# Order of high and low weight parts, and modulation sums of two column groups per call, in a two-block transformer kernel

## The chip, the cores and the metric

One core of a Trainium2 chip runs one program of about 39,000 instructions. The metric is the device time of one execution in microseconds, the median of the runs shown. A profile holds one execution.

## What is computed

The reference runs two blocks on 256 tokens of width 2048, in float32. The first block has two layers and a second stream, the context, of 256 tokens as well. In each layer the input is scaled and shifted by a modulation that comes from a vector `c` (for the tokens) and `c_ctx` (for the context):

```python
sh_l, sc_l, g_l = jnp.split(jax.nn.silu(c) @ w_mod[l] + b_mod[l], 3, axis=-1)
sh_c, sc_c, g_c = jnp.split(jax.nn.silu(c_ctx) @ w_mod[l] + b_mod[l], 3, axis=-1)
hl = xl * (1.0 + sc_l[:, None, :]) + sh_l[:, None, :]
parts_l = jnp.split(hl @ w_in[l], SPLIT_POINTS, axis=-1)
```

Then come a short convolution, differential attention and a pooling, a product with `w_out`, a residual gated by `g_l` or `g_c`, and a layer norm. The second block has a norm, two attentions of eight heads, gated products `w_proj_a`, `w_proj_b` and `w_out`, and a feed-forward part with `w_up` and `w_down` of width 8192.

## The kernel before

The weights are streamed from HBM once, in chunks of 512 KB: two row blocks of 128 (`CHUNK = 2`) by 512 columns, or four row blocks by 256. `fetch` (line 169) issues the transfer on SP's queue, lets ACT copy the chunk to a high part in float32r (line 184) and DVE subtract to get the low part (line 185). Two chunks are made ahead of the one in use (`LOOKAHEAD`); raw, high and low tiles have three buffers each. A product of float32 accuracy is the sum of three float32r products: high by high, high by low, low by high.

Two functions multiply. `lin_b` (line 250) takes the weights as the stationary operand and gives the result transposed, four blocks of 128 columns in four accumulators. With 256 tokens it folds the two products of the high weights into one: high and low parts of the activations stand side by side as 512 columns, so each row block of each column block is a product of 512 columns (line 266) and one of 256 columns with the low weights (line 268), one after the other. With 512 tokens it calls `mm3` (line 245), three products of 512 columns. `lin_a` (line 278) takes the activations as the stationary operand and the weights as the moving one, with `mm3` as well: 512 columns, or 256 in the last two column blocks of `w_out` and of the last `w_down`. In the second layer and the second block nearly all of `lin_b` is folded. The first layer works on 512 tokens.

The order of the chunks is one list, `stream`, filled ahead of the work by `plan` and `weave` (lines 145 and 148). `weave` puts chunks of the modulation's weights `w_mod` between those of the main products: one by one in the first layer, one for three in the second. `side` (line 195) runs twice per chunk; it hands modulation chunks to their step function and counts down the list `deferred`, whose entries run when their count reaches zero. `bg_step` advances attention and norms between chunks.

The first column groups of the first layer's modulation go through PE directly (`mod_first`, line 365). All others go through `mod_side` (line 403), a job of one group `nt` of 512 columns. For each row of a chunk DVE multiplies by the column of `silu(c)` and adds into an accumulator `ma0` for the context and `ma1` for the tokens (lines 416 and 418). When the last chunk is done, `deferred` holds `cols` for shift and scale or `gate` for the gate, due after five calls of `side`. Both sum over the 128 partitions by a product with a 128 by 32 tile of ones, one per stream, into rows 0 to 31 and 32 to 63 of one tile `aux` (lines 428 and 446). `cols` copies 64 rows back (line 430), and two calls later `finish` transposes four blocks of 128 columns on PE (line 435) and sets the columns (line 436). `gate` loads 64 rows of `b_mod` on ACT's queue (line 442), adds it on DVE stream by stream (line 448) and writes one row per stream to HBM (line 449).

The jobs are: two single groups for the first layer's scale and shift (line 909), four gate groups of both streams for the first layer (`side0`), eight scale and shift groups for the second (`side1`, in the order of `NTS`, line 456), and four gate groups of the token stream alone (`side2`). The accumulators have one buffer each. A tile of the pool `qs` (ten buffers of 544 columns) serves input pieces, high and low parts of the heads, the pooling and four rows of the forget gate. Its column sums lie in a tile `fc` of its own (line 1157).

Of the kernel before, what the change touches and what calls it, by code (L numbers as in the profile page):

```python
# [12 lines left out]
F32 = mybir.dt.float32  # L13
# [48 lines left out]
def tile_two_blocks(ctx: ExitStack, tc: tile.TileContext, a: dict, out: bass.AP, blocks: dict):  # L62
# [14 lines left out]
    p_qs = pool("qs", 10)  # L77
# [167 lines left out]
    def mm3(ps, lh, ll, rh, rl, start, stop):  # L245
        mm(ps, lh, rh, start=start, stop=False)  # L246
        mm(ps, lh, rl, start=False, stop=False)  # L247
        mm(ps, ll, rh, start=False, stop=stop)  # L248

    def lin_b(act, tok, consume, ncols=512, korder=K16, mid=None):  # L250


        ntok = tok.stop - tok.start
        fold = 2 * ntok == 512
        nb = [(b * P, min(P, ncols - b * P)) for b in range((ncols + P - 1) // P)]
        ps = [acc() for _ in nb]
        for k0 in korder:
            hi, lo = wget()
            last = k0 == korder[-1]
            nk = hi.shape[1]  # L260
            for (c, w), p in zip(nb, ps):
                for kk in range(nk):
                    ah, al = act[k0 + kk]
                    start, stop = k0 == korder[0] and kk == 0, last and kk == nk - 1
                    if fold:
                        mm(p[:w, :].rearrange("p (a t) -> p a t", a=2), hi[:, kk, c:c + w], act.both(k0 + kk, tok),  # L266
                           start=start, stop=False)
                        mm(p[:w, :ntok], lo[:, kk, c:c + w], ah[:, tok], start=False, stop=stop)  # L268
                    else:
                        mm3(p[:w, :ntok], hi[:, kk, c:c + w], lo[:, kk, c:c + w], ah[:, tok], al[:, tok], start, stop)  # L270
                if last:
                    consume(c // P, (p[:w].rearrange("p (a t) -> p t a", a=2),) if fold else p[:w, :ntok])
            side()
            bg_step()
            if mid:
                mid(k0)

    def lin_a(act, tiles, consume, korder=K16, mid=None, hold=1, lead=0, hook=None):
# [4 lines left out]
        for ks in [korder[:lead]][:lead] + [[k] for k in korder[lead:cut]] + [korder[cut:]]:  # L283
# [119 lines left out]
    def mod_side(l, nt, streams=(0, 1), wait=5):  # L403

        st = {}

        def fn(k0):
            def step(raw):
                if k0 == 0:
                    for s in streams:  # L410
                        st[s] = p_ma.tile([P, 512], F32, tag=f"ma{s}", name=f"ma{s}")
                for kk in range(CHUNK):
                    k = k0 + kk
                    for s in streams:
                        if k == 0:
                            V.tensor_scalar(st[s], raw[:, kk, :], cc2[:, k, s:s + 1], None, op0=ALU.mult)
                        else:
                            V.scalar_tensor_tensor(st[s], raw[:, kk, :], cc2[:, k, s:s + 1], st[s], op0=ALU.mult,  # L418
                                                   op1=ALU.add)
                if k0 == K16[-1]:  # L420
# [3 lines left out]

        def cols():
            ps = aux()
            for s in streams:
                mm(ps[32 * s:32 * s + 32, :], ones, st[s], start=True, stop=True)
            r = st[0][:64]
            S.copy(r, ps[:64])  # L430

            def finish():
                pt = aux()[:, :256].rearrange("p (b r) -> p b r", b=4)
                for b in range(4):
                    nc.tensor.transpose(pt[:, b, :], r[:, b * P:(b + 1) * P], ident[:64, :64])
                set_cols(l, nt // 4, nt % 4 * 4, 4, pt.rearrange("p b (s t) -> p b s t", s=2)[:, :, :, 0])
            deferred.append([2, finish])

        def gate():
            o = (nt - 8) * 512  # L440
            br = tmp()
            S.dma_start(br[:64], bass.AP(tensor=a["b_mod"].tensor, offset=a["b_mod"].offset + l * 3 * D + 2 * D + o,
                                         ap=[[0, 64], [1, 512]]))
            ps = aux()
            for s in streams:
                mm(ps[32 * s:32 * s + 32, :], ones, st[s], start=True, stop=True)
            for s in streams:
                V.tensor_add(br[32 * s:32 * s + 32], ps[32 * s:32 * s + 32, :], br[32 * s:32 * s + 32])
                S.dma_start(grow[l][s:s + 1, o:o + 512], br[32 * s:32 * s + 1])
        return entries(("w_mod", l), nt * 512, 512, K16, fn)  # L450


# [3 lines left out]
    NTS = [nt for j in range(4) for nt in (j, 4 + j)]  # L456
# [446 lines left out]
    for j, (kt, n) in enumerate(GROUPS):  # L903
        w = [e for name, g in L_FIRST for e in entries(("w_in", 0), O[name] + 512 * g, 512, range(kt, kt + n, CHUNK),
                                                   nk=min(n, CHUNK))]
        if j + 1 < len(GROUPS):
            nxt = GROUPS[j + 1]
            if n == 4:
                m0, m1 = mod_side(0, nxt[0] // 4, wait=2), mod_first(1, *nxt, ("act",))
# [232 lines left out]
    fc = cst.tile([P, T], F32, name="fc")  # L1142
# [275 lines left out]
```

## Time and profile before

| | us |
|---|---|
| median of 3 runs | 2888.54 |
| lowest and highest | 2886.82, 2889.2 |
| the profiled execution | 2888.59 |
| its span, first to last instruction | 2886.8 |

| engine | busy us | share |
|---|---|---|
| PE, matmuls | 2857.0 | 99% |
| PEld, weight loads | 2371.6 | 82% |
| DVE | 2003.2 | 69% |
| ACT | 1159.7 | 40% |
| POOL | 222.5 | 8% |

PE is TensorE, DVE VectorE, ACT ScalarE, POOL GpSimd, SP SyncE. A row of the timeline has the start in us, the duration in us, engine, line, operation, output and inputs, the shape (stationary operand by moving operand) and a count. The end of a matmul is modelled and overlaps the start of the next one, so the pace is read from starts. A row of one line gives the count, the least, median and greatest duration in ns and the starts of the first and the last instruction in the stretch.

### The profile page before, as it was taken

Reading aid. Unit: us, or ns where it says so; the run is one execution under the profiler, and the core shown is the slowest. Engines: PE = TensorE matmul, PEld = TensorE weight load, DVE = VectorE, ACT = ScalarE, POOL = GpSimd, SP = SyncE. Lnnn points to the kernel's source line nnn. Section 1 sums busy time; section 2 is a strip of 40 time slices with the busy share of each in tenths; the row PEclk is TensorE's granted clock in tenths of the full one; section 3 lists DMA queues with packets and bytes.
Section 4 is the critical chain, followed back from the end, with each engine's and each line's share of the span. In section 5 each row is a group of like instructions: output and inputs, shape, how many; then the busy total and the mean of one; then the engine's idle time right before and its main releaser. Section 6 shows DMA issues by size and latency. Waiting matters only on the chain.

```text
span 2886.8 us, 39022 instructions
## 1 busy us (share of the span) xinstructions
PE 2857.0 (99%) x14970; PEld 2371.6 (82%) x14970; DVE 2003.2 (69%) x3061; ACT 1159.7 (40%) x1620; POOL 222.5 (8%) x284
## 2 busy tenths in 40 slices
PE   8999999999999999999999999999999999999998
PEld 6777787777879788888888888888888888888887
DVE  5889987887975658467676666776656656565564
ACT  3223432432312435245445443544444444344443
POOL 0000001001100410011100000001101001010011
PEclk9999999999999999999999999999999999999999
DMA  9764455445764445445756555455656656656555
GB/s 332 275 211 142 135 173 165 147 163 178 246 197 134 135 137 194 157 161 192 244 168 194 182 157 188 156 188 184 204 183 189 191 189 188 194 181 196 190 188 168
DMA packets 150532, 533.89 MB, mean 185 GB/s; under 512 B 17204, under 2 KB 21052, under 8 KB 149320
## 3 DMA queue, kind: packets, MB, share of 16 engines
q1 hardware_dynamic: 142752, 510.79, 54.3%
q0 software_dynamic: 5632, 18.36, 2.1%
q10 hardware_dynamic: 1960, 2.24, 0.3%
q8 instruction: 117, 1.92, 0.3%
q14 instruction: 71, 0.58, 0.1%
HBM read 527.09 MB, written 4.23 MB: 184 GB/s over the span
## 4 chain that ended last, share of the span: by engine, by line
PE 76%; DVE 2%; issue 2%; DMA 1%; ACT 1%; POOL 0%; POOLq 0%; ACTq 0%; DVEq 0%
PE acc L266 23%; PE acc L246 12%; PE acc L248 12%; PE acc L247 12%; PE acc L268 12%; PE aux L670 1%; PE aux L702 1%; DVE lo L185 1%; DVE ma L418 1%; PE aux L692 0%; PE aux L1184 0%; ACT hi L184 0%; DMA raw<-in_w_in_dram 0%; DMA raw<-in_w_out_dram 0%; PE aux L1214 0%
## 5 line engine op out<-in xcount | busy, mean ns | idle before, releaser
L185 DVE TENSOR_TENSOR lo<-raw,hi 128x1024 fp32r<-128x1024 f32 (+1 forms) x774 | 947.0, 1226 | 646.3 <-ACT hi L184 645.2
L184 ACT CAST hi<-raw 128x1024 fp32r<-128x1024 f32 (+1 forms) x774 | 808.4, 1045 | 1419.1 <-PE acc L248 447.8
L266 PE MATMUL acc<-act,hi 128*128 128x512 f32 x2960 | 1048.1, 399 | 0.4 <-DVE qs L308 0.4
L268 PE MATMUL acc<-act,lo 128*128 128x256 f32 x2960 | 828.3, 280 | 0.0
L266 PEld LDWEIGHTS acc<-act,hi 128*128 128x128 f32 x2960 | 554.1, 187 | 139.7 <-issue 5.1
L246 PE MATMUL acc<-hi,act 128*128 128x512 f32 (+1 forms) x1568 | 584.2, 373 | 2.7 <-ACT act L350 1.7
L247 PE MATMUL acc<-lo,act 128*128 128x512 f32 (+1 forms) x1568 | 578.6, 369 | 1.1 <-DVE lo L185 1.1
L248 PE MATMUL acc<-hi,act 128*128 128x512 f32 (+1 forms) x1568 | 578.6, 369 | 0.1
L268 PEld LDWEIGHTS acc<-act,lo 128*128 128x128 f32 x2960 | 556.9, 188 | 1.9 <-DVE lo L185 0.3
L418 DVE SCALAR_TENSOR_TENSOR ma<-mod,cc,ma 128x512 f32<-128x512 f32 x480 | 339.5, 746 | 26.2 <-DMA mod<-in_w_mod_dram 24.8
L246 PE MATMUL acc<-act,hi 128*128 128x512 f32 x896 | 356.9, 398 | 0.2 <-ACT hi L184 0.2
L247 PE MATMUL acc<-act,hi 128*128 128x512 f32 x896 | 350.2, 391 | 0.0
L248 PE MATMUL acc<-act,lo 128*128 128x512 f32 x896 | 350.1, 391 | 0.0
L246 PEld LDWEIGHTS acc<-hi,act 128*128 128x128 f32 x1568 | 296.5, 189 | 56.9 <-issue 4.0
L248 PEld LDWEIGHTS acc<-hi,act 128*128 128x128 f32 x1568 | 296.2, 189 | 51.5 <-DVE act L351 1.5
L247 PEld LDWEIGHTS acc<-lo,act 128*128 128x128 f32 x1568 | 296.6, 189 | 50.5 <-DVE lo L185 2.5
L246 PEld LDWEIGHTS acc<-act,hi 128*128 128x128 f32 x896 | 168.6, 188 | 46.1 <-issue 8.8
L248 PEld LDWEIGHTS acc<-act,lo 128*128 128x128 f32 x896 | 168.5, 188 | 35.9 <-issue 0.4
L247 PEld LDWEIGHTS acc<-act,hi 128*128 128x128 f32 x896 | 168.7, 188 | 33.5 <-issue 0.5
L317 DVE TENSOR_REDUCE tmp<-acc 128x256 f32<-128x512 f32 x185 | 124.3, 684 | 57.3 <-PE acc L268 57.3
L1292 POOL TENSOR_TENSOR tmp<-tmp 128x256 f32<-128x256 f32 x64 | 53.0, 828 | 573.3 <-DVE tmp L1291 566.6
L678 ACT ACTIVATE pp<-aux,small 128x512 f32<-128x512 f32 (+1 forms) x96 | 58.3, 613 | 55.1 <-DVE small L674 55.0
(217 smaller groups left out, 1655.0 us busy)
## 6 DMA issues: line engine op xcount, KB each, us to landing
raw<-in_w_in_dram SPq DMA_DIRECT2D x379, 512.0 KB, 4.0
mod<-in_w_mod_dram SPq DMA_DIRECT2D x152, 512.0 KB, 3.7
raw<-in_w_up_dram SPq DMA_DIRECT2D x128, 512.0 KB, 4.1
raw<-in_w_down_dram SPq DMA_DIRECT2D x128, 512.0 KB, 4.2
raw<-in_w_out_dram SPq DMA_DIRECT2D x96, 512.0 KB, 4.3
mod<-in_w_mod_dram SPq DMA_DIRECT2D x8, 2048.0 KB, 13.5
raw<-in_w_proj_a_dram SPq DMA_DIRECT2D x16, 512.0 KB, 4.1
raw<-in_w_proj_b_dram SPq DMA_DIRECT2D x16, 512.0 KB, 4.3
```

Source lines behind the costliest of these rows:

```text
L184: S.copy(hi, raw)
L185: (fn or V).tensor_sub(lo, raw, hi)
L246: mm(ps, lh, rh, start=start, stop=False)
L247: mm(ps, lh, rl, start=False, stop=False)
L248: mm(ps, ll, rh, start=False, stop=stop)
L266: mm(p[:w, :].rearrange("p (a t) -> p a t", a=2), hi[:, kk, c:c + w], act.both(k0 + kk, tok), start=start, stop=False)
L268: mm(p[:w, :ntok], lo[:, kk, c:c + w], ah[:, tok], start=False, stop=stop)
L317: V.reduce_sum(t, ps[0], axis=AX.X)
L418: V.scalar_tensor_tensor(st[s], raw[:, kk, :], cc2[:, k, s:s + 1], st[s], op0=ALU.mult, op1=ALU.add)
L670: mm(p[:, :nk], a[r, q0:q0 + P], b[r, 0:nk], start=n == 0, stop=n == 2)
L678: S.activation(t, ps[i][:, :nk], AF.Exp, bias=nm[:, i:i + 1], scale=QK_SCALE, accum_out=sums[:, i:i + 1])
L1292: G.tensor_mul(t, t, t)
```

## The change

In `lin_b` and `lin_a` the products of a chunk that use the high weights come first and those that use the low weights last. In `lin_b` this goes over all column blocks in the middle chunks and by column block in the first and the last chunk. `mod_side` takes a list of column groups; their accumulators stay until the last group's last chunk, and then one call sums up to four of them, on rows 0 to 127 of `aux`, followed by one copy, four transposes and one `set_cols` per group. Gates are paired as (8, 9) and (10, 11), scale and shift of the second layer as (j, 4 + j). The two single groups of the first layer stay single. The pool `qs` has nine buffers, and `fc` uses the accumulator `ma0`.

```diff
-    p_qs = pool("qs", 10)
+    p_qs = pool("qs", 9)
...
-    def mm3(ps, lh, ll, rh, rl, start, stop):
-        mm(ps, lh, rh, start=start, stop=False)
-        mm(ps, lh, rl, start=False, stop=False)
-        mm(ps, ll, rh, start=False, stop=stop)
...
-            for (c, w), p in zip(nb, ps):
-                for kk in range(nk):
-                    ah, al = act[k0 + kk]
-                    start, stop = k0 == korder[0] and kk == 0, last and kk == nk - 1
-                    if fold:
-                        mm(p[:w, :].rearrange("p (a t) -> p a t", a=2), hi[:, kk, c:c + w], act.both(k0 + kk, tok),
-                           start=start, stop=False)
-                        mm(p[:w, :ntok], lo[:, kk, c:c + w], ah[:, tok], start=False, stop=stop)
-                    else:
-                        mm3(p[:w, :ntok], hi[:, kk, c:c + w], lo[:, kk, c:c + w], ah[:, tok], al[:, tok], start, stop)
-                if last:
-                    consume(c // P, (p[:w].rearrange("p (a t) -> p t a", a=2),) if fold else p[:w, :ntok])
+
+            pairs = list(zip(nb, ps))
+            for g in ([[x] for x in pairs] if last or k0 == korder[0] else [pairs]):
+                for (c, w), p in g:
+                    for kk in range(nk):
+                        ah, al = act[k0 + kk]
+                        wt, start = hi[:, kk, c:c + w], k0 == korder[0] and kk == 0
+                        if fold:
+                            mm(p[:w, :].rearrange("p (a t) -> p a t", a=2), wt, act.both(k0 + kk, tok), start=start,
+                               stop=False)
+                        else:
+                            mm(p[:w, :ntok], wt, ah[:, tok], start=start, stop=False)
+                            mm(p[:w, :ntok], wt, al[:, tok], start=False, stop=False)
+                for (c, w), p in g:
+                    for kk in range(nk):
+                        mm(p[:w, :ntok], lo[:, kk, c:c + w], act[k0 + kk][0][:, tok], start=False,
+                           stop=last and kk == nk - 1)
+                    if last:
+                        consume(c // P, (p[:w].rearrange("p (a t) -> p t a", a=2),) if fold else p[:w, :ntok])
...
+                    tt, p = slice(t * P, (t + 1) * P), ps[i][:, :n]
                     for kk in range(nk):
-                        ah, al = act[k0 + kk]
-                        mm3(ps[i][:, :n], ah[:, t * P:(t + 1) * P], al[:, t * P:(t + 1) * P], hi[:, kk], lo[:, kk],
-                            k0 == korder[0] and kk == 0, k0 == korder[-1] and kk == nk - 1)
+                        for j, x in enumerate(act[k0 + kk]):
+                            mm(p, x[:, tt], hi[:, kk], start=k0 == korder[0] and kk == j == 0, stop=False)
+                    for kk in range(nk):
+                        mm(p, act[k0 + kk][0][:, tt], lo[:, kk], start=False, stop=k0 == korder[-1] and kk == nk - 1)
...
-    def mod_side(l, nt, streams=(0, 1), wait=5):
+    def mod_side(l, nts, streams=(0, 1), wait=5):
+        jobs = [(nt, s) for nt in nts for s in streams]
...
+                        j = jobs.index((nt, s))
+                        st[nt, s] = p_ma.tile([P, 512], F32, tag=f"ma{j}", name=f"ma{j}")
...
+                if (nt, k0) == (nts[-1], K16[-1]):
                     deferred.append([wait, cols if nt < 8 else gate])
...
+        n = 32 * len(jobs)
+        def sums():
+            ps = aux()
+            for j, job in enumerate(jobs):
+                mm(ps[32 * j:32 * j + 32, :], ones, st[job], start=True, stop=True)
+            return ps
         def cols():
-            ps = aux()
-            for s in streams:
-                mm(ps[32 * s:32 * s + 32, :], ones, st[s], start=True, stop=True)
-            r = st[0][:64]
-            S.copy(r, ps[:64])
+            ps = sums()
+            r = st[jobs[0]][:n]
+            S.copy(r, ps[:n])
             def finish():
-                pt = aux()[:, :256].rearrange("p (b r) -> p b r", b=4)
+                pt = aux()[:, :4 * n].rearrange("p (b r) -> p b r", b=4)
                 for b in range(4):
-                    nc.tensor.transpose(pt[:, b, :], r[:, b * P:(b + 1) * P], ident[:64, :64])
+                    nc.tensor.transpose(pt[:, b, :], r[:, b * P:(b + 1) * P], ident[:n, :n])
...
         def gate():
...
+            for j, (nt, s) in enumerate(jobs):
+                o = (nt - 8) * 512
+                S.dma_start(br[32 * j:32 * j + 32],
+                            bass.AP(tensor=a["b_mod"].tensor, offset=a["b_mod"].offset + l * 3 * D + 2 * D + o,
+                                    ap=[[0, 32], [1, 512]]))
+            ps = sums()
+            V.tensor_add(br[:n], ps[:n], br[:n])
...
-    side0 = [e for nt in range(8, 12) for e in mod_side(0, nt)]
-    side1 = [e for nt in NTS for e in mod_side(1, nt)]
-    side2 = [e for nt in range(8, 12) for e in mod_side(1, nt, (1,))]
+    side0 = [e for nt in (8, 10) for e in mod_side(0, (nt, nt + 1))]
+    side1 = [e for j in range(4) for e in mod_side(1, (j, 4 + j))]
+    side2 = [e for nt in (8, 10) for e in mod_side(1, (nt, nt + 1), (1,))]
...
-    fc = cst.tile([P, T], F32, name="fc")
+    fc = p_ma.tile([P, 512], F32, tag="ma0", name="fc")[:, :T]
```

## Rows read from the trace of the kernel before

**Rows 1.** Page, part 1: busy time, share of the span, count of each engine.

```profile
PE 2857.0 (99%) x14970; PEld 2371.6 (82%) x14970; DVE 2003.2 (69%) x3061; ACT 1159.7 (40%) x1620; POOL 222.5 (8%) x284
```

**Rows 2.** Waits of PE: engine line waited for, total us, times, longest us.

```profile
PE aux L670 <- ACT pp L678: 2.0, 1, 2.0
...
PE acc L247 <- DVE lo L185: 1.1, 2, 0.9
```

**Rows 3.** Busy time of each engine in one stretch, us.

```profile
core 0: us, PE busy (x) PEld busy (x) DVE busy (x) ACT busy (x) POOL busy (x), PEclk, DMA share, GB/s
200.00:300.00 100.00, 99.00 (x455) 77.97 (x454) 96.03 (x177) 35.24 (x56) 5.78 (x8) 1.00 0.47 149
```

**Rows 4.** Line 248 in a stage of 512-column products, w_down of group 0.

```profile
L248 PE MATMUL acc<-hi,act x128: 389/389/398, 2257.2 to 2343.6; 128*128 128x512 f32 x128
```

**Rows 5.** Timeline of PE, 512 then 256 columns: start, us, engine, line, instruction.

```profile
2854.39 0.39 PE L248 MATMUL acc<-hi,act 128*128 128x512 f32 x1
2854.62 0.28 PE L246 MATMUL acc<-hi,act 128*128 128x256 f32 x1
...
2854.85 0.28 PE L248 MATMUL acc<-hi,act 128*128 128x256 f32 x1
...
2857.49 0.28 PE L246 MATMUL acc<-hi,act 128*128 128x256 f32 x1
```

**Rows 6.** Line 268 in two stretches of the alternating order.

```profile
L268 PE MATMUL acc<-act,lo x256: 277/281/284, 2344.1 to 2434.2; 128*128 128x256 f32 x128
...
L268 PE MATMUL acc<-act,lo x148: 274/277/280, 1898.9 to 1949.9; 128*128 128x256 f32 x148
```

**Rows 7.** Timeline of PE where 512-column products follow 256-column ones.

```profile
2434.30 0.40 PE L246 MATMUL acc<-hi,act 128*128 128x512 f32 x1
...
2434.77 0.39 PE L248 MATMUL acc<-hi,act 128*128 128x512 f32 x1
...
2435.69 0.39 PE L246 MATMUL acc<-hi,act 128*128 128x512 f32 x1
```

**Rows 8.** Calls of sums: two in the chain, two in the timeline of PE.

```profile
547.19 0.98 PE aux L428 x4
...
1363.78 0.97 PE aux L446 x2
...
1167.25 1.05 PE L446 MATMUL aux<-ma,ones 128*32 128x512 f32 x2
1168.22 0.50 PE L246 MATMUL acc<-hi,act 128*128 128x512 f32 x1
1168.56 0.39 PE L247 MATMUL acc<-lo,act 128*128 128x512 f32 x1
...
171.71 1.92 PE L379 MATMUL aux<-mod,csil 128*32 128x512 f32 x16
173.56 0.50 PE L246 MATMUL acc<-act,hi 128*128 128x512 f32 x1
```

**Rows 9.** Timeline of PE: four transposes from 64 rows, four from 128.

```profile
136.30 0.39 PE L248 MATMUL acc<-act,lo 128*128 128x512 f32 x1
136.62 0.46 PE L435 MATMUL aux<-ident,ma 64*128 64x64 f32 x4
137.01 0.50 PE L246 MATMUL acc<-act,hi 128*128 128x512 f32 x1
...
653.05 0.60 PE L718 MATMUL aux<-ident,tmp 128*128 128x128 f32 x4
653.40 0.48 PE L246 MATMUL acc<-act,hi 128*128 128x512 f32 x1
```

**Rows 10.** Groups by line: count, busy us, mean ns, idle before.

```profile
L266 PE MATMUL acc<-act,hi 128*128 128x512 f32 x2960 | 1048.1, 399 | 0.4 <-DVE qs L308 0.4
...
L428 PE MATMUL aux<-ma,ones 128*32 128x512 f32 x40 | 10.5, 603 | 0.0
...
L446 PE MATMUL aux<-ma,ones 128*32 128x512 f32 x24 | 8.4, 604 | 0.0
```

More of the change, by code (lines that the diff above doesn't have):

```diff
@@ L401, in mod_first, with fn @@
         return res
-    def mod_side(l, nt, streams=(0, 1), wait=5):
+    def mod_side(l, nts, streams=(0, 1), wait=5):
+        jobs = [(nt, s) for nt in nts for s in streams]
         st = {}
-        def fn(k0):
+        def fn(nt, k0):
             def step(raw):
@@ L414, in step @@
                     for s in streams:
+                        t = st[nt, s]
                         if k == 0:
-                            V.tensor_scalar(st[s], raw[:, kk, :], cc2[:, k, s:s + 1], None, op0=ALU.mult)
+                            V.tensor_scalar(t, raw[:, kk, :], cc2[:, k, s:s + 1], None, op0=ALU.mult)
                         else:
-                            V.scalar_tensor_tensor(st[s], raw[:, kk, :], cc2[:, k, s:s + 1], st[s], op0=ALU.mult,
-                                                   op1=ALU.add)
-                if k0 == K16[-1]:
+                            V.scalar_tensor_tensor(t, raw[:, kk, :], cc2[:, k, s:s + 1], t, op0=ALU.mult, op1=ALU.add)
+                if (nt, k0) == (nts[-1], K16[-1]):
                     deferred.append([wait, cols if nt < 8 else gate])
@@ L437, in cols @@
+                for i, nt in enumerate(nts):
+                    set_cols(l, nt // 4, nt % 4 * 4, 4,
+                             pt.rearrange("p b (i s t) -> p i b s t", s=2, t=32)[:, i, :, :, 0])
             deferred.append([2, finish])
         def gate():
-            o = (nt - 8) * 512
             br = tmp()
-            S.dma_start(br[:64], bass.AP(tensor=a["b_mod"].tensor, offset=a["b_mod"].offset + l * 3 * D + 2 * D + o,
-                                         ap=[[0, 64], [1, 512]]))
@@ L444, in gate @@
[L444 to L450, printed above, removed]
+            for j, (nt, s) in enumerate(jobs):
[3 more added lines that the diff above has]
+                                    ap=[[0, 32], [1, 512]]))
@@ L453, in tile_two_blocks @@
+            ps = sums()
+            V.tensor_add(br[:n], ps[:n], br[:n])
+            for j, (nt, s) in enumerate(jobs):
+                o = (nt - 8) * 512
+                S.dma_start(grow[l][s:s + 1, o:o + 512], br[32 * j:32 * j + 1])
+        return [e for nt in nts for e in entries(("w_mod", l), nt * 512, 512, K16, lambda k0, nt=nt: fn(nt, k0))]
     O = dict(cu=0, cb=512, cc=1024, cg=1536, q=2048, k=3072, v=4096, ag=5120, pu=6144, pg=6656)
@@ L455, in tile_two_blocks @@
     L_REST = [("cc", 0), ("v", 1), ("k", 1), ("q", 1), ("ag", 1), ("cb", 0), ("cg", 0), ("pu", 0), ("pg", 0)]
-    NTS = [nt for j in range(4) for nt in (j, 4 + j)]
     GROUPS = [(0, 1), (1, 1), (2, 2), (4, 4), (8, 4), (12, 4)]
@@ L908, in tile_two_blocks @@
             if n == 4:
-                m0, m1 = mod_side(0, nxt[0] // 4, wait=2), mod_first(1, *nxt, ("act",))
+                m0, m1 = mod_side(0, (nxt[0] // 4,), wait=2), mod_first(1, *nxt, ("act",))
                 m = m0[:4] + m1[:1] + m0[4:] + m1[1:]
```

2 lines of the change are left out of this document (removed).

## The prediction

> **What bounds the kernel now.** I read the engines' shares first: PE is busy 99% of the span, DVE 69%, ACT 40% [rows 1]. Matmul ends are modelled, so that share alone proves little. The second view is who waited for whom on PE: the longest single wait after the start is 2.0 us, and all waits for a low part come to 1.1 us [rows 2]. The third is the stretch by engine: even where DVE is fullest, 96%, PE is busy 99% [rows 3]. So PE's own stream is the bound nearly everywhere. What takes time there is the distance from one matmul's start to the next one's, and that I took from first and last starts.
>
> In a stage of 512-column products alone 128 rounds of three stand between 2257.2 and 2343.6, which is 86.4 / 127 / 3 = 0.2268 us a step [rows 4]. In a run of 256-column products 23 starts span 2854.85 to 2857.49, 0.1200 us a step [rows 5]. A high and a low product at those two steps are 0.3468 us. The alternating order of `lin_b` (512, 256, 512, 256) needs 90.1 / 255 = 0.3533 us a pair in one whole stage and 51.0 / 147 = 0.3469 us in another stretch [rows 6]. Three more whole stages of 256 pairs ran at the slow step; I take two thirds slow, a mean of 0.351. That is the slack part 1 can touch.
>
> **Part 1, order of high and low.** No product, weight load or column is added or removed: 2960 pairs before and after [rows 10]. Of their chunks 268 are middle ones (42 products of 8 chunks with 6 each, 8 of 4 chunks with 2 each) and 100 are first or last.
>
> A middle chunk becomes eight 512-column products and then eight of 256. At the pure steps that is 8 x 0.3468 = 2.774 us. Two changes of shape come with it. Into 256 columns the first two steps take 0.23 us instead of 0.24 [rows 5], so 0.01 is gained. Back into 512 the first six take 1.39 us, 2434.30 to 2435.69 [rows 7], against 6 x 0.2268 = 1.36, so 0.03 is lost. Net 2.794 us, against 8 x 0.351 = 2.808 now: 0.014 x 268 = 3.8 us gained. Bounds: if all pairs already ran at 0.3469, the switches lose 0.02 x 268 = 5.4 us; if the switches were free, 0.034 x 268 = 9.1 are gained. I take the middle, since both switches stand in the trace.
>
> A first or last chunk goes by column block, two of 512 and two of 256. Two 512s after a switch take 0.47 us [rows 7], two 256s 0.23 [rows 5], together 0.70 against 0.702 now. 400 such blocks give 0.8 us gained, with bounds of 2.6 lost and 3.4 gained.
>
> With four or more high products ahead of it, a low part that is late no longer stops PE. The waits that can go are 1.1 us [rows 2]; I take 1. What is late next is the high part, which ACT makes and this order does not help. A high buffer now comes free after 8 of 16 products, so ACT's next cast may start up to a microsecond earlier; the low buffer is held to the chunk's end as before. No engine gets more work, and I cost that at nothing.
>
> In `lin_a` and in the 512-token products of the first layer all steps are 512 columns (or 256) whatever the order, so the order costs nothing there; the bounds are the waits just named.
>
> **Part 2, sums of the modulation.** There are 18 calls of the sums now: 10 of two streams (40 records in pairs of passes) and 8 gates, of which 4 have two streams and 4 one (24 records) [rows 10]. After it there are 10: 2 single column groups of the first layer, 4 pairs of the second layer, 2 + 2 pairs of gates. Eight fall away.
>
> Each lasts 0.98 us with two streams and 0.97 with one [rows 8], so the streams run side by side. Around it the stream loses more: entering a narrower shape takes 0.32 us instead of 0.227 [rows 9], and the first product behind takes 0.34 (1168.22 to 1168.56) instead of 0.227 [rows 8]. Alone a call thus costs 0.97 + 0.09 + 0.11 = 1.17 us, beside other auxiliary work 0.98. I take 1.1: 8 x 1.1 = 8.8 us gained, bounds 7.8 and 9.4.
>
> Four streams in a call should cost what two do. Eight products on four quadrants, 16 records, take 173.56 - 171.71 = 1.85 us [rows 8], two batches of about 0.93. So nothing is added. The Trainium skill, page TensorE: Matmul & The Clock Gate, section Measured speedup vs the span model, lists 3.07 times for four row tiles, not 4; by it a call of four would be longer by a third, and six such calls would give back some 2 us as an estimate. The row shows no such loss, and I go by it.
>
> The transposes behind go from ten groups to six. Such a group now takes 0.39 us (136.62 to 137.01), enters late by 0.09 [rows 9] and leaves by 0.11, 0.59 together. A group on 128 rows, as the four new ones will be, takes 0.35 (653.05 to 653.40) and needs no narrower shape on the way in [rows 9]; with the exit 0.46. So 10 x 0.59 - 2 x 0.59 - 4 x 0.46 = 2.9 us gained.
>
> Elsewhere: DVE's gate additions go from 12 to 4, ACT's copies from 10 to 6; both lie beside PE and are worth nothing while PE bounds. ACT issues 12 loads of b_mod instead of 8, in front of the hi casts queued behind them; the gate's addition waits for the last, and the low parts stand behind it on DVE. The cover is two chunks made ahead. Between nothing and one worst wait of 2.0 us [rows 2] for each of four gates I take 0.5 us lost. The first column group of a pair waits eight chunks longer for its sums, but the last pair ends where the last group did, and only it is awaited. The next accumulators wait for the transposes half as often. The ninth instead of tenth qs buffer and the shared tile for fc are reused long after their last readers; a head's four tiles take those of two heads before. I cost them at nothing; with that cover gone, a wait of 2.0 us at each of the two pooling stages, 4 us.
>
> **The sum.** 3.8 + 0.8 + 1 + 8.8 + 2.9 - 0.5 = 16.8 us less. The profiled execution took 2888.59 us, 1.8 beyond its span of 2886.8, and stands 0.05 above the median of the three runs. 2888.6 - 16.8 = 2871.8, so **2872 us**.
>
> **Rivals.** *The order doesn't matter to the step* (0.19): the present 0.353 comes from something else, such as where the weights lie, and remains. For it: the same alternating order ran at 0.347 too, without any change in code. Then part 1 gives only its 1 us: 2888.6 - 12.2 = 2876. The Trainium skill, same page, section Back-to-back issue gap, has N / 2.4 + 2.5 ns for a warm step, which no order changes; 216 and 109 ns by that rule, and the rows here are above it.
>
> *Runs without a price for the switch* (0.15): all 2960 pairs go at 0.3468, 12.4 us instead of 4.6: 2864. For it: one of the two switches gains. Against: the 0.03 us back into 512 columns.
>
> *The freed time becomes waits* (0.13): the calls of the first layer lie where DVE is fullest, up to 96% [rows 3]. PE would wait for lo parts instead. Then part 2 is lost and part 1 remains, 2888.6 - 5.1 = 2883.5. Against: there too PE waits for low parts 1.1 us at most [rows 2].
>
> *Slower: each change between runs drains PE* (0.07). Place: the switch between high and low run. If it cost what entering and leaving the narrow shape do, 0.1 us [rows 8, 9], 268 x 2 + 100 x 8 = 1336 switches are 134 us, less the 12.4 and the other 12.2: about 2998. The sign turns at 24.6 / 1336 = 18 ns a switch. Against: the rows give -10 and +30 ns, a mean of 10, and the +30 is cut short where a run has two products.
>
> *The change doesn't do what it says*: four quadrants are not side by side and six calls keep their double length. That gives 6 us back, 2878; 0.06, and it lies within the range.
>
> **How the numbers follow.** The forecast has 0.40; its own range is 2863 to 2880 from the bounds above. 0.2% is about what a measurement of this kernel can tell from no change, 5.8 us: faster is under 2882.8. Forecast, the neutral order, the free switch and the serial quadrants all lie there, with 0.80. The lost time counts as no change, 0.13. The drained switch is slower, 0.07. The range goes from the free switch with a slow step everywhere before, 2960 x 0.0065 = 19.2 and the other 12.2 (2857), to the case of lost time and a microsecond or two beyond (2885).
>
> **What would show it.** In the profile after: a step of about 0.227 inside eight high and 0.120 inside eight low products of a middle chunk; w_up stages of 256 pairs shorter than 90.1 us by about half a microsecond; 10 calls of sums, of the same 0.98 us; six groups of transposes; no wait for lo on PE. The forecast is wrong if the first steps of each run are far over 0.24 us, if a call on four quadrants takes over 1.2, or if waits for ACT's hi, DVE or aux appear where the calls were.

## The result, and the profile after the change

The changed kernel took a median of 2873.85 us (2871.32 to 2876.18, 4 runs), beside 2888.87 for the kernel before on the same chip: a ratio of 0.9949, 95% interval 0.9932 to 0.9966, 15.0 us less. 2872 was forecast, in a range of 2857 to 2885. In the third set of experiments it ran again: 2871.10 (5 runs) beside 2887.70, ratio 0.9937 [0.9923, 0.995], 16.6 less. So the total of 16.8 came out. Several of its terms did not, as the traces and the runs below show. The profiled execution of the first set is the longest of its four, 2876.18 us; that of the third is the second shortest of its five, 2867.47.

The page of the changed kernel, part 1, answers to [rows 1]: PE's busy time is 20 us less with nearly the same count, and DVE has as much to do as before.

```profile
PE 2836.9 (99%) x14954; PEld 2373.3 (83%) x14954; DVE 2006.9 (70%) x3053; ACT 1156.3 (40%) x1618; POOL 217.9 (8%) x284
```

The order, in the timeline of PE in a w_up stage, two middle chunks (start, length, line, and how many instructions the row holds):

```profile
2345.56 2.00 PE L264 MATMUL acc<-act,hi 128*128 128x512 f32 x8
2347.40 1.11 PE L271 MATMUL acc<-act,lo 128*128 128x256 f32 x8
2348.35 2.00 PE L264 MATMUL acc<-act,hi 128*128 128x512 f32 x8
2350.19 1.12 PE L271 MATMUL acc<-act,lo 128*128 128x256 f32 x8
```

From one run of eight highs to the next it is 2348.35 - 2345.56 = 2.79 us a chunk, where 2.794 was forecast: 1.84 for the highs and 0.95 for the lows. The low products of a whole w_up stage and of the stretch that had run fast before, by line:

```profile
L271 PE MATMUL acc<-act,lo x256: 274/283/283, 2334.9 to 2423.6; 128*128 128x256 f32 x128
...
L271 PE MATMUL acc<-act,lo x146: 274/283/283, 1889.3 to 1939.7; 128*128 128x256 f32 x146
```

The stage needs 88.7 us between its first and last low product, where it was 90.1 [rows 6]; the other row needs 50.4 for 146 pairs, 0.348 a pair, where it was 0.347. What ran slowly gained, and what ran fast lost a little.

The sums and the transposes behind them, in PE's timeline, a pair of column groups of the second layer and its transposes, answer to [rows 8, 9]:

```profile
659.21 1.06 PE L437 MATMUL aux<-ma,ones 128*32 128x512 f32 x8
660.21 0.50 PE L267 MATMUL acc<-act,hi 128*128 128x512 f32 x1
660.55 0.39 PE L268 MATMUL acc<-act,hi 128*128 128x512 f32 x1
...
665.79 0.60 PE L448 MATMUL aux<-ident,ma 128*128 128x128 f32 x4
666.15 0.48 PE L267 MATMUL acc<-act,hi 128*128 128x512 f32 x1
666.46 0.40 PE L268 MATMUL acc<-act,hi 128*128 128x512 f32 x1
```

Four streams take 660.21 - 659.21 = 1.00 us; two took 0.98 [rows 8]. The first product behind takes 0.34, as before. The transposes from 128 rows take 0.36, and 0.31 for the first product behind.

PE's waits in the changed kernel, whole span (engine, line, what it waited for: total us, times, longest us):

```profile
PE aux L651 <- DVE tmp L647: 6.8, 2, 4.5
...
PE aux L685 <- ACT pp L693: 3.3, 2, 2.7
```

No wait for a low part (L185) is left in the whole list. The first row is new: the pool product of `do_pu` waits for DVE, 2.3 us in the first layer's pooling stage and 4.5 in the second's; in the kernel before it was 0.8 us, once, in the second:

```profile
PE aux L636 <- DVE tmp L632: 0.8, 1, 0.8
```

The row L685 is the attention's wait of [rows 2] at its new line.

The second layer's pooling stage grew from 63.8 us (1344.1 to 1407.9) to 68.2 (1332.4 to 1400.6). It is counted here, in every kernel, over the last 320 products into `acc` ahead of the next stage (the second half of `do_cg`, then `do_pu` and `do_pg`), from the start of the first of them to the first product of the next stage. Waits of DVE and POOL in that stretch:

```profile
DVE tmp L646 <- DMA tmp<-in_invc_dram: 5.1, 2, 4.7
...
POOL qs L628 <- DVE tmp L646: 12.7, 1, 12.7
```

In the kernel before, DVE's wait for the factors is shorter there, and POOL has none at the pads:

```profile
DVE tmp L631 <- DMA tmp<-in_invc_dram: 1.0, 1, 1.0
```

By line, the loads of the averaging factors (643, from issue to landing), the clearing of the pads (628) and the row loads (865); the landing in us, the others in ns of the shortest, median and longest, then first and last start in us:

```profile
DMA to landing us min/median/max: 3.8/3.8/8.8
...
L628 POOL MEMSET qs<- x3: 105/124/124, 1357.8 to 1370.6; 128x8 f32 x3
...
L865 POOL DMA_DIRECT2D p<-in_ln_g_dram x4: 538/538/538, 1370.9 to 1372.5; - x4
```

In the kernel before the same three clearings went out within 0.2 us:

```profile
L613 POOL MEMSET qs<- x3: 125/127/128, 1367.8 to 1368.0; 128x8 f32 x3
...
L850 POOL DMA_DIRECT2D p<-in_ln_g_dram x4: 538/538/538, 1368.0 to 1369.6; - x4
```

With nine buffers one pad has to wait until DVE's multiplication has read the old buffer. POOL stands at it for 12.7 us, and the row loads queued behind go out 38.5 us into the stage, not 24. There they overlap the factors' loads in time, one of which takes 8.8 us to land; DVE waits for it, and PE for DVE.

### The profile page after: what moved, and what is told of

The parts are those of the page before. It is cut to its first block, busy times and chain, and to the rows that moved or that the text cites. A ratio compares the mean times of both kernels' runs of the same rounds, so it can differ in the third digit from the quotient of the medians.

```text
span 2874.4 us, 39003 instructions
## 1 busy us (share of the span) xinstructions
PE 2836.9 (99%) x14954; PEld 2373.3 (83%) x14954; DVE 2006.9 (70%) x3053; ACT 1156.3 (40%) x1618; POOL 217.9 (8%) x284
## 4 chain that ended last, share of the span: by engine, by line
PE 85%; DVE 7%; DMA 3%; issue 3%; ACT 1%; POOL 0%; SPq 0%; POOLq 0%; ACTq 0%; DVEq 0%
PE acc L264 23%; PE acc L297 20%; PE acc L271 17%; PE acc L299 10%; PE acc L267 6%; PE acc L268 6%; DMA mod<-in_w_mod_dram 2%; DVE ma L426 2%; DVE lo L185 1%; PE aux L685 1%; PE aux L717 1%; PE aux L383 1%; PE aux L707 1%; DVE small L687 0%; DMA tmp<-in_invc_dram 0%
## 5 line engine op out<-in xcount | busy, mean ns | idle before, releaser
L185 DVE TENSOR_TENSOR lo<-raw,hi 128x1024 fp32r<-128x1024 f32 (+1 forms) x774 | 950.9, 1232 | 663.9 <-ACT hi L184 591.4
L264 PE MATMUL acc<-act,hi 128*128 128x512 f32 x2960 | 800.0, 395 | 0.1
L297 PE MATMUL acc<-hi,act 128*128 128x512 f32 (+1 forms) x3136 | 768.9, 370 | 2.5 <-ACT act L354 1.4
L271 PE MATMUL acc<-act,lo 128*128 128x256 f32 (+1 forms) x3856 | 709.2, 307 | 0.0
L271 PEld LDWEIGHTS acc<-act,lo 128*128 128x128 f32 x3856 | 612.9, 189 | 92.4
L297 PEld LDWEIGHTS acc<-hi,act 128*128 128x128 f32 x3136 | 548.3, 189 | 104.5 <-ACT hi L184 3.0
L264 PEld LDWEIGHTS acc<-act,hi 128*128 128x128 f32 x2960 | 509.2, 188 | 74.8 <-issue 1.5
L299 PE MATMUL acc<-lo,act 128*128 128x512 f32 (+1 forms) x1568 | 438.3, 368 | 0.1
L267 PE MATMUL acc<-act,hi 128*128 128x512 f32 x896 | 358.7, 400 | 0.2 <-ACT hi L184 0.2
L268 PE MATMUL acc<-act,hi 128*128 128x512 f32 x896 | 352.4, 393 | 0.0
L267 PEld LDWEIGHTS acc<-act,hi 128*128 128x128 f32 x896 | 169.7, 189 | 44.1 <-issue 7.7
L268 PEld LDWEIGHTS acc<-act,hi 128*128 128x128 f32 x896 | 169.9, 190 | 34.3 <-issue 0.7
L785 DVE TENSOR_TENSOR p<-acc,p 128x512 f32<-128x512 f32 x100 | 66.3, 685 | 12.4 <-PE acc L271 11.3
L355 DVE TENSOR_TENSOR act<-tmp,act 128x256 fp32r<-128x256 f32 (+1 forms) x107 | 67.6, 638 | 5.0 <-ACT act L354 5.0
L354 ACT CAST act<-tmp 128x256 fp32r<-128x256 f32 (+1 forms) x107 | 50.4, 478 | 38.5 <-POOL tmp L1307 21.7
```

What stands on the lines that cost most here:

```text
L185: (fn or V).tensor_sub(lo, raw, hi)
L264: mm(p[:w, :].rearrange("p (a t) -> p a t", a=2), wt, act.both(k0 + kk, tok), start=start, stop=False)
L267: mm(p[:w, :ntok], wt, ah[:, tok], start=start, stop=False)
L268: mm(p[:w, :ntok], wt, al[:, tok], start=False, stop=False)
L271: mm(p[:w, :ntok], lo[:, kk, c:c + w], act[k0 + kk][0][:, tok], start=False, stop=last and kk == nk - 1)
L297: mm(p, x[:, tt], hi[:, kk], start=k0 == korder[0] and kk == j == 0, stop=False)
```

## Experiments

All times are medians, beside the kernel before on the same chip in the same set (2888.27, 2887.53 and 2887.70 us in sets one to three). "Stage" is the second layer's pooling stage.

### The two parts alone

The order alone: `lin_b` and `lin_a` of the changed kernel in the kernel before.

```diff
-                        mm3(ps[i][:, :n], ah[:, t * P:(t + 1) * P], al[:, t * P:(t + 1) * P], hi[:, kk], lo[:, kk],
...
+                        for j, x in enumerate(act[k0 + kk]):
+                            mm(p, x[:, tt], hi[:, kk], start=k0 == korder[0] and kk == j == 0, stop=False)
+                    for kk in range(nk):
+                        mm(p, act[k0 + kk][0][:, tt], lo[:, kk], start=False, stop=k0 == korder[-1] and kk == nk - 1)
```

> Part 1 alone; sums, ten qs buffers and fc as before. Against the kernel before: by the forecast's step sum 5 to 6 us faster; if the slow alternating step of 0.353 is the commoner one, as the trace after suggests (w_up stages of 89.2 us instead of 90.3), up to 9 faster. If the order doesn't matter to the step, at most 1 us faster. No wait of the pooling stage for DVE of more than 1 us, since the qs buffers are ten.

Measured: 2881.09 (11 runs), ratio 0.9978 [0.9969, 0.9986], 7.2 us less, between the two numbers expected. Of the five stages of 256 pairs behind the second pooling stage four are 1.1 us shorter; the fifth, at 2166.5 in the kernel before, ran at the fast step there and is 0.4 longer. The stretch behind the wait for a low part at 968.8 gains 3.0. The two kernels there, by windows (us, PE busy, PEld, DVE, ACT, POOL, granted clock, DMA share, GB/s), first before, then the order alone:

```profile
970.00:974.00 4.00, 4.00 (x14) 3.16 (x13) 4.00 (x5) 2.03 (x5) 4.00 (x3) 0.68 0.85 287
```

```profile
968.00:972.00 4.00, 4.00 (x23) 3.41 (x22) 4.00 (x5) 3.00 (x5) 4.00 (x3) 1.00 0.61 196
```

Before, PE had waited 1.14, 0.94 and 0.88 us in a row, for ACT, a high and a low part; then the granted clock was at its lower level (1.2 GHz), with products 0.43 us apart from 969.1 to 972.5 instead of 0.23, as its timeline shows:

```profile
967.41 0.49 PE L246 MATMUL acc<-hi,act 128*128 128x512 f32 x1 [0.94 <-ACT hi L184]
968.78 0.52 PE L247 MATMUL acc<-lo,act 128*128 128x512 f32 x1 [0.88 <-DVE lo L185]
969.12 0.61 PE L248 MATMUL acc<-hi,act 128*128 128x512 f32 x1
969.53 0.63 PE L246 MATMUL acc<-hi,act 128*128 128x512 f32 x1
...
972.52 0.41 PE L247 MATMUL acc<-lo,act 128*128 128x512 f32 x1
```

With the order alone only 0.3 us of wait for the high part is left there and the clock stays at 1.00: 0.9 and 0.6 of waits and eight products at 0.2 us less make up the 3.0. The pooling stage lost 4.3 us in this kernel too, though it has ten buffers and no wait there of more than 1 us was expected: DVE waits 3.1 us for the factors, PE 2.7 for DVE. POOL waits at no pad here, the row loads go out after 25.5 us, and the factor in question lands 3.3 us after its issue. So this stage can lose as much without the ninth buffer's wait.

```profile
DVE tmp L635 <- DMA tmp<-in_invc_dram: 3.1, 1, 3.1
```

The sums alone: the changed kernel with the old loops of `lin_b` and `lin_a`, nine buffers.

```diff
-                        for j, x in enumerate(act[k0 + kk]):
-                            mm(p, x[:, tt], hi[:, kk], start=k0 == korder[0] and kk == j == 0, stop=False)
...
+                        mm3(ps[i][:, :n], ah[:, t * P:(t + 1) * P], al[:, t * P:(t + 1) * P], hi[:, kk], lo[:, kk],
```

> Part 2 alone with its nine qs buffers; products in the old order. By the forecast 11 to 12 us faster. If the nine buffers cost the pooling stages what the trace after shows there (waits of 4.5 and 2.5 us), 5 to 8 faster. If freed time in the first layer becomes waits, 0 to 3 faster.

Measured: 2880.01 (11 runs), 0.9978 [0.9969, 0.9987], 8.3 less, just above the 5 to 8 that were expected with the pooling stages' waits. PE's wait for the pool product is 7.2 us in two, and the stage is 5.9 longer. The two parts add up: 7.2 + 8.3 = 15.5, the change gave 15.0 and 16.6.

### What a call of sums costs

Eight calls more, whose sums nothing reads, in the changed kernel with the pads on DVE (next section).

```diff
+                    if len(nts) > 1:
+                        deferred.append([wait - 2, sums])
                     deferred.append([wait, cols if nt < 8 else gate])
```

> The kernel of e3_pads with eight more calls of the sums, one ahead of each paired call; their results are not read. If a call costs its 1.1 us on PE's path: 8 to 9 us slower than e3_pads, so some 12 faster than the kernel before. If PE's time there is filled by waits for DVE anyway: less than 3 us slower.

Measured: 2874.36 (5 runs), 0.9952 [0.9939, 0.9966], 6.0 us more than the same kernel without them in this set (2868.32), between the two numbers expected. By line there are 56 records more than 64, with the same length:

```profile
L439 PE MATMUL aux<-ma,ones x120: 592/593/617, 133.0 to 1353.3; 128*32 128x512 f32 x120
```

That is 0.75 us a call, 0.9 against the same kernel's median of 2867.01 in the first set, for a call that occupies PE for 1.0 us. A likely reason is that part of a call falls into waits of PE that are there anyway: the waits at the pool products are 1.8 us in this profile and 4.0 without the calls. It is not shown, since the wait for DVE at line 312, which reads a finished accumulator, is longer here, 3.5 us against 1.9. Nor is the forecast's lower bound of 7.8 ruled out: single executions of the two kernels lie 5.1 and 3.3 us apart. The forecast's 1.1 a call looks like too much, no more.

### The pooling stage

The clearing of the pads on DVE instead of POOL, in the changed kernel:

```diff
-                G.memset(u[:, :, 0:8], 0.0)
-                G.memset(u[:, :, 264:272], 0.0)
+                V.memset(u[:, :, 0:8], 0.0)
+                V.memset(u[:, :, 264:272], 0.0)
```

> The changed kernel, but the pads of the pooling's tiles are set by DVE instead of POOL, so that POOL's row loads do not stand behind a wait for the ninth buffer. If that wait moves the row loads onto the load of the pooling's factors: 3 to 6 us faster than the changed kernel, 18 to 21 faster than the one before, and the factors land within 5 us. If the late factors were chance: as the changed kernel, 15 faster than before.

Measured: 2867.01 (5 runs), 0.9933 [0.992, 0.9945], 21.3 less than before, as in the first of the two cases, though one of the factors took 6.6 us to land and not under 5. The row loads go out 26 us into the stage, which takes 64.6. Waits of that stage, of PE and DVE, and then the row loads by line:

```profile
PE aux L651 <- DVE tmp L647: 1.0, 1, 1.0
...
DVE tmp L646 <- DMA tmp<-in_invc_dram: 1.4, 1, 1.4
```

```profile
L865 POOL DMA_DIRECT2D p<-in_ln_g_dram x4: 536/536/538, 1352.1 to 1353.7; - x4
```

The same kernel again, in the second set:

> The kernel of e3_pads once more, on the same chip as the three beside it: 18 to 22 us faster than the kernel before.

Measured: 2868.32 (5 runs), 0.9933 [0.992, 0.9945], 19.2 less. The stage took 66.1, with PE waiting 1.9 us for DVE's `put`, which reads a finished accumulator, and 1.6 at the pool product. Ten runs of two sets are all between 2865.7 and 2869.7; the nine of the changed kernel lie between 2867.2 and 2876.2. The intervals of the ratios overlap; the means, 2867.8 and 2872.1, are 4.3 apart. A gain of 3 to 6 us is likely but not proven by the ratios alone.

The same edit in the kernel before, ten buffers:

> The kernel before (ten qs buffers, old order, old sums) with the pads of the pooling's tiles set by DVE. If e3_pads gained because nine buffers made POOL wait: within 1.5 us of before. If POOL's wait for the pads costs as much with ten buffers: 4 to 7 us faster than before.

Measured: 2887.97 (11 runs), 1.0001 [0.9992, 1.001], no change. With ten buffers POOL has no wait there to be rid of.

Nine buffers alone, in the kernel before:

```diff
-    p_qs = pool("qs", 10)
+    p_qs = pool("qs", 9)
```

> The kernel before with nine qs buffers instead of ten, nothing else. If the ninth buffer is what makes the pooling stage wait: 2 to 6 us slower than before, and POOL waits over 5 us at its third pair of pads in the second layer. If not: within 1 us of before.

Measured: 2887.34 (11 runs), 1.0002 [0.9993, 1.0011]. The time misses, the trace does not: the stage is 69.2 us, 5.4 longer, POOL waits 15.2 us at the pads and PE 5.6 at the pool product.

```profile
POOL qs L613 <- DVE tmp L631: 15.2, 1, 15.2
```

Ahead of this stage, however, the kernel is 5.1 us earlier: with a buffer less the program's order of ACT's, DVE's and PE's work in the attention is another, and the slow stretch of the granted clock behind 511.6 and the one behind 969 are gone. In this profile one gain hid the other loss.

The second of these stretches is not the buffers' doing alone. The waits ahead of it are the same as in the kernel before, 1.14, 0.94 and 0.87 us, and the products behind them follow at 0.23 us:

```profile
966.14 0.50 PE L247 MATMUL acc<-lo,act 128*128 128x512 f32 x1 [0.87 <-DVE lo L185]
966.48 0.39 PE L248 MATMUL acc<-hi,act 128*128 128x512 f32 x1
966.71 0.40 PE L246 MATMUL acc<-hi,act 128*128 128x512 f32 x1
```

Of the five profiles with the old order three have the slow stretch there (the kernel before, with the pads on DVE too, and the sums alone); this one and the next have the waits without it.

Both edits in the kernel before, nine buffers and the pads on DVE:

> The kernel before with nine qs buffers and the pads of the pooling tiles cleared on DVE. Theory (nine buffers make DVE wait at the second layer's pooling, the clearing on POOL behind that wait holds back the row loads, and this pooling stage then loses about 5 us; the gain of about 5 us that the nine buffers bring earlier is a thing apart): with the clearing off POOL the stage is back at 64 to 65 us and the gain stays, so 3 to 6 us faster than before, 2882 to 2885. Rival (the nine buffers only shift time about): within 2 us of before, as with the pads on POOL.

Measured: 2886.36 (11 runs), 0.9995 [0.9986, 1.0004]. In time this is the rival's result. In the trace the stage is 65.2 us, 4.0 less than with nine buffers alone, and the 5.0 gained ahead of it are there too. But the profiled execution, the shortest of the eleven, ends 3.5 ahead of the kernel before, and the medians are only 1.3 apart.

The order alone, ten buffers, the pads on DVE:

> The order of high and low parts alone, ten qs buffers, the pads on DVE. With the pads on POOL it was 7.2 us faster than before and lost 4.3 us in the second layer's pooling stage. Theory (that loss is the pads' place behind the wait): 10 to 12 us faster than before, 2876 to 2878. Rival (the loss is that of a stage that starts earlier and finds its loads no earlier): 6 to 8 us faster, 2880 to 2882.

Measured: 2879.86 (6 runs), 0.9969 [0.9958, 0.998], 7.8 less: the rival's number. The stage is 65.7 us instead of 68.1, which the gains, 0.6 apart, don't show. So by the medians the pads' place matters in the whole change and hardly in the parts tried; nine buffers and the new sums with the old order were not tried.

At last the factors themselves: in the changed kernel with the pads on DVE, all four of the second layer loaded once at the stage's start, into two accumulators of the sums that are idle there.

```diff
+            ics = []
+            if not both:
+                for j in range(2):
+                    t = p_ma.tile([P, 512], F32, tag=f"ma{2 + j}", name=f"ma{2 + j}")
+                    S.dma_start(t, bass.AP(tensor=a["invc"].tensor, offset=a["invc"].offset + j * 512, ap=[[0, P], [1, 512]]))
+                    ics += [t[:, :T], t[:, T:]]
...
-                ic = tmp(T)
-                S.dma_start(ic, bass.AP(tensor=a["invc"].tensor, offset=a["invc"].offset + b * T,
+                if ics:
+                    ic = ics[b]
```

> The changed kernel with the pads on DVE, and the second layer's pooling factors loaded once, at the stage's start, into two accumulators that are idle there, instead of a tile for each block amid the row loads. Theory (what is left of the wait at this stage is DVE waiting for these factors): 1 to 4 us faster than the same kernel without it, 2864 to 2867, and no wait of DVE for the factors there. Rival (the raw chunks and row loads bind there): within 1 us of it, 2867 to 2869.

Measured: 2866.00 (4 runs), 0.9923 [0.991, 0.9937], 21.7 less, the fastest here. No wait of DVE for the factors is left in the stage, none of PE at the pool product; it takes 62.9 us, less than before the change. PE's waits in it:

```profile
PE acc L264 <- DVE qs L312: 0.8, 2, 0.6
```

Beside the changed kernel of the same set it is 5.1 us faster; against the pads on DVE, of other sets, by 1.0 and 2.3, which the intervals don't separate. By this trace DVE's wait for the factors is what bound there; what its removal is worth in time beyond the pads is not settled.

The changed kernel again, in that set:

> The changed kernel as it is, again, beside the other three on one chip: 14 to 16 us faster than before, 2872 to 2875, with the wait of about 4 us or more for DVE in the second layer's pooling stage, if its cause is in the program and not in one run.

Measured: 2871.10 (5 runs), the ratio given above, a little less time than expected. PE's wait at the pool product of the second layer is there again, shorter, 3.1 us, and the stage takes 66.4. The profiled execution was 8.7 us shorter than the first one (spans 2865.7 and 2874.4) with the same program. Two places of the first layer make up 6.8 of that, here in windows of the first execution (its attention, then its pooling) and the same of the second:

```profile
502.00:506.00 4.00, 1.89 (x8) 1.14 (x7) 4.00 (x9) 0.06 (x1) 0.00 (x0) 1.00 0.72 258
506.00:510.00 4.00, 3.44 (x11) 2.74 (x12) 4.00 (x9) 1.89 (x5) 0.00 (x0) 0.51 0.50 153
...
716.00:720.00 4.00, 2.03 (x8) 1.00 (x6) 4.00 (x6) 2.73 (x5) 0.00 (x0) 1.00 0.39 131
720.00:724.00 4.00, 3.66 (x8) 2.48 (x9) 4.00 (x7) 1.19 (x2) 0.00 (x0) 0.64 0.76 225
```

```profile
502.00:506.00 4.00, 4.00 (x21) 3.25 (x22) 4.00 (x9) 1.18 (x3) 0.00 (x0) 1.00 0.40 130
...
708.00:712.00 4.00, 2.84 (x11) 1.69 (x9) 4.00 (x7) 3.04 (x5) 0.00 (x0) 1.00 0.26 60
712.00:716.00 4.00, 2.80 (x11) 2.00 (x12) 4.00 (x6) 1.45 (x3) 0.00 (x0) 1.00 0.71 230
```

DVE is full in all of them. In the attention PE waits 2.7 us in the first execution, and the clock is low behind it; in the second that wait is not there. In the pooling stage PE waits 2.3 us for the pool product in both, and only in the first is the clock low behind it.

### Runs as short as a column block

A step of the prediction on trial: the order by column block (two highs, two lows) in the middle chunks as well, with four times the switches. In the changed kernel with the pads on DVE:

```diff
-            for g in ([[x] for x in pairs] if last or k0 == korder[0] else [pairs]):
+            for g in [[x] for x in pairs]:
```

> The kernel of e3_pads with the middle chunks in the order of the first and last ones: two high, two low products per column block, so four changes of shape back and forth per chunk instead of one. If a change of shape costs what the rows show (a middle chunk 2.794 us, four blocks 2.786), within 2 us of e3_pads, rather faster. If each change cost 18 ns or more, as the rival for slower has it, 268 chunks x 6 more changes x 18 ns = 29 us slower than e3_pads.

Measured: 2875.86 (5 runs), 0.9958 [0.9946, 0.9971], 7.5 more than without the edit; neither expected number came out. The switches are not the cause: in the timeline a pair of pairs takes 0.69 or 0.70 us, four of them 2.79, as much as a chunk in long runs.

```profile
2360.21 0.63 PE L264 MATMUL acc<-act,hi 128*128 128x512 f32 x2
...
2360.91 0.63 PE L264 MATMUL acc<-act,hi 128*128 128x512 f32 x2
...
2362.30 0.63 PE L264 MATMUL acc<-act,hi 128*128 128x512 f32 x2
```

PE waits instead, more than in long runs. By the profiles four of the five stages of 256 pairs are 1.6 us longer than without the edit, and the pooling stage takes 69.5 us, where it took 64.6 and 66.1. Two rows of PE's list have grown, the first in the pooling stage and the second in those four stages (without the edit they are 0.9 and 1.9 for the first and nothing for the second), and the timeline at one place shows the second:

```profile
PE acc L264 <- DVE qs L312: 4.8, 2, 4.3
PE acc L264 <- DVE tmp L321: 3.6, 12, 0.3
```

```profile
2350.53 1.05 ACT L184 CAST hi<-raw 128x1024 fp32r<-128x1024 f32 x1 [1.74 <-PE acc L264]
...
2352.06 1.22 DVE L185 TENSOR_TENSOR lo<-raw,hi 128x1024 fp32r<-128x1024 f32 x1
...
2355.64 0.68 DVE L321 TENSOR_REDUCE tmp<-acc 128x256 f32<-128x512 f32 x1
2356.37 0.73 PE L264 MATMUL acc<-act,hi 128*128 128x512 f32 x2 [0.30 <-DVE tmp L321]
```

ACT's cast waits until PE is done with the high buffer, which in this order is at the chunk's end; the low part then falls on DVE among the four reads of the finished accumulators, and the next product waits for the third of them, which ends at 2356.32. In long runs the four reads go off from 2346.08 to 2350.20 with the low part behind them. Why the alternating order, which also holds the high buffer to the end, has no such wait in the kernel before is open.

## Why the prediction was right, and where its steps were not

**Middle, first and last chunks** (forecast 3.8 + 0.8 less). The pitch came out to the last digit, 2.79 us a chunk. Behind the second pooling stage lie six folded stages, five of 256 pairs and one of 1040. Together, each from its first main product to the next stage's, they take 829.2 to 832.8 us in the five profiles with the old order and 826.5 to 827.3 in seven with the new one (without the extra calls and the short runs): 4.7 less in the mean. From the kernel before to the two executions of the changed one it is 5.4 and 5.5. The whole stretch from the end of that pooling stage to the last main product, which has more than these pairs in it, is 5.5 us shorter in the changed kernel's first profile (it is 7.4 ahead of the kernel before at 1407.9 and 12.8 at 2877.5), 4.3 in its second, 3.3 with the order alone and 5.6 with the order and the pads on DVE. The sign named, "about half a us" a w_up stage, was too small for four stages, which had run at 0.3533: 1.1 between stages, 1.4 by the rows. The mean of 0.351 had taken in stretches at the fast step, which lose.

**Waits for low parts** (1 less). At 968.8 it is 1.5 of waits, a high part's 0.6 among them, and 3.0 where the slow stretch of the granted clock behind them goes as well, which [rows 2] can't show. That stretch was not in every execution with these waits, so 1.5 is what the order itself takes away. A list of waits counts the idle time alone.

**Calls** (8.8 less). On PE as forecast, 1.00 us for four streams. Eight calls put back cost 6.0 to 7.3 in the medians, under the lower bound of 7.8, which their scatter does not rule out. On column tiles, four streams in 1.00 us against one in 0.97 [rows 8] are 3.9 times one. The Trainium skill (TensorE: Matmul & The Clock Gate, Measured speedup vs the span model) lists 3.07 for four row tiles and 2.38 for three column tiles; the trace shows no such loss.

**Transposes** (2.9 less). By the rows as forecast, 0.36 for the group and 0.08 to leave; not measured alone.

**Gate loads** (0.5 more). No wait for them stands in PE's list of the changed kernel.

**Nine buffers and fc** (nothing, or 4 us more with the cover gone). This is the step that failed: the cost was put at nothing. The second layer's pooling stage grew by 4.4 us and, in the second profile, by 2.6; the first layer's has a wait of 2.3 us that was not there. "Reused long after their last readers" was true of a head's four tiles and not of the pads, and the price was not only PE's wait but POOL's queue behind it: row loads 14 us later, into the factors' loads. The ninth buffer is not all of it, since the order alone, with ten buffers, lost 4.3 us in the same stage; the stage had no cover to spare, and what the ninth buffer and what the earlier start take of it is not separated. In the first layer it looks like the rival *the freed time becomes waits*, at one place: DVE is full there, and PE, sooner at its product, waits. Neither nine buffers alone nor the order alone has that wait; the sums with nine buffers have it, with 2.0 us. The pads are not its reason: with them on DVE it is 2.4 us.

So 4.7, 1.5 to 3.0, 6.0 to 7.3 and 2.9 make 15 to 18 us gained; 2.6 to 4.4 in the second pooling stage and 2.3 to 4 in the first's, with the slow products behind the wait, are 5 to 8 lost. That leaves 7 to 13, and 15.0 and 16.6 were measured. The rest I can't attribute to a term. Nine buffers alone gained 5 us ahead of the second pooling stage, by another order of the engines' work and by a clock that did not fall at 969, and that is the likeliest place; no run took it apart. The total came out by luck in part: the terms of the order and of the calls' length held, errors of both signs met in the rest.

Of the **rivals**, the neutral order falls with the pitch, and the drain with the pitch of long runs and of blocks alike. Runs without a price for the switch would be 2.774 a chunk; the runs of eight show 2.79. Serial quadrants fall with the 1.00 us of four streams.

## What to carry to other kernels

A buffer taken from a pool is paid for where a slow queue stands in line for it: look for which instruction takes the freed buffer next, and what is queued behind it on its engine, loads above all. A wait of PE should be priced with the products that follow it, which may run at the lower clock in one execution and not in the next. A term should be read from several executions of either kernel, since two of one program differ by more than most terms here.

## What was not expected of the hardware

Alternating 512- and 256-column products ran at 0.3533 us a pair in some stages and 0.3469 in others [rows 6], while runs of eight and of two come to 0.349 and pure stretches to 0.347. It does not go with the code of a stage. The stage at 2166.5 of the kernel before, behind some transposes at its start, ran at 76.7 / 221 = 0.347 to its end. The same stage of the same kernel with the pads on DVE ran at 33.0 / 95 = 0.347 in its first half and at 44.2 / 125 = 0.354 in its second, with no other instruction on PE in between:

```profile
L268 PE MATMUL acc<-act,lo x222: 274/280/282, 2180.0 to 2256.7; 128*128 128x256 f32 x111
```

```profile
L268 PE MATMUL acc<-act,lo x96: 274/280/282, 2180.8 to 2213.8; 128*128 128x256 f32 x96
...
L268 PE MATMUL acc<-act,lo x126: 277/281/284, 2213.8 to 2258.0; 128*128 128x256 f32 x126
```

So the alternating order can go over from one step to the other inside a stage. What makes it do so is open.

Two executions of one program had spans 8.7 us apart, 0.3%. In the first layer's pooling PE waited 2.31 us in one and 2.36 in the other, and the granted clock fell to its lower level behind the one and not behind the other. At the lower level a 512-column product took 0.43 us, as the timeline from 969.12 on shows; the Trainium skill (TensorE: Matmul & The Clock Gate, Back-to-back issue gap) has 512 / 1.2 = 427 ns, which agrees. At the upper level it has 216 ns, and the rows show 227.
